# Output projection of a hybrid encoder layer as seven block products, with combinations of the operands formed by GpSimd

## The chip, the cores and the metric

The kernel runs on one NeuronCore of one Trainium2 chip. The metric is the device time in microseconds of one execution. Before the change it is 1117.38 us, the median of three runs (1113.78 to 1118.88).

The engines have their short names: PE is TensorE, DVE is VectorE, ACT is ScalarE, POOL is GpSimd, SP is SyncE. In this kernel nearly all transfers are issued by SP, whose instruction stream is in order: a transfer that must wait for something holds back all those written behind it.

## The reference

One layer on x of 1024 tokens by 1024 features, all in fp32. A combined input projection of the RMS-normalised x feeds three token mixers (a convolution module, a bidirectional retention, and a multi-head latent attention of 8 heads). Their outputs stand side by side, 2048 wide, and are gated. The part that matters here is the end:

```
mix = concat(conv, retention, attention) * silu(gate)     # 1024 tokens x 2048
x   = x + mix @ w_out                                      # w_out: 2048 x 1024
out = rmsnorm(x, final_g)
```

## The kernel before

A matmul of fp32 data is made of three: `mm3` (L174 to 177) splits each operand into a high part, which ACT makes as a cast, and a low part, which DVE makes as the difference, and multiplies high by high, low by high and high by low. So each operand that comes from DRAM costs a transfer on SP, a cast on ACT and a subtraction on DVE before PE can use it.

The kernel has three stages. First the input projection, with the convolution and the retention in its shadow. Then, from about 542 to 943 us, the attention: 16 units (`Unit`, L797 to 863; the loop is L914 to 964), one for each head and each half of the 512 + 512 query tokens, of some 25 us. A unit multiplies queries and keys (L813 to 817), takes the softmax (L820 on DVE, L822 on ACT), transposes the probabilities on PE (`tr`, L831; ACT's cast PH at L833 and DVE's PL empty the bank) and multiplies them by the values (`pvs`). `slot_plan` (L882) puts the projections of the next heads' queries, keys and values between these steps; among them is the rotary part of two heads' queries, `g_r` and `g_r2` (L753 to 776): SP copies rows of `xr` to `xs`, POOL does two multiplications and an addition, ACT casts the result `xh`.

The end of a unit runs while the next one is on. `norm` (L836) loads the gate rows `g`, transposes the softmax sums, stores them to DRAM (`rs_dram`, L846), loads them back broadcast (`rb`, L848), and lets POOL multiply `g` by `rb`. `fin` (L860) lets DVE multiply the unit's result in the bank `pv` by `g` into `osb`, and SP stores it to `y_dram`. `y_dram` holds the transposed mix as 16 tiles of 128 features by 1024 tokens; tiles 0 to 7 are from the convolution and the retention and are complete before the attention, tiles 8 to 15 belong to the 8 heads.

Last comes the output projection (L917 to 1061). `wo_load` loads a tile of w_out (512 KB), casts and splits it; all 16 tiles stay in SBUF. `y_load` loads half of a tile of the mix (256 KB), casts and splits it. There are 8 row tiles of 128 tokens (`st`), 2 column halves, 16 tiles of the contraction and 3 matmuls each: 768 matmuls of 128x512 (of the last row tile one half is cut in two). The first 4 row tiles are started while loads are still coming, and some of their matmuls already stand among the last unit's. `finish` (L1018) adds x, normalises, and stores a row tile.

The order of the instructions on each engine is not the order of the code: when the program is built, a list scheduler with a simulated timeline puts them in order, and the order is then fixed. On the chip each engine goes through its own list and waits on semaphores. Buffers come from pools; `bufs=n` of a tag gives n of them in turn, and a tile waits for the last reader of the one n before it.

## Time and profile before

| | |
|---|---|
| median of three runs | 1117.38 us |
| the profiled execution | 1115.57 us |
| its span in the trace | 1113.8 us |
| mean granted clock of PE | 0.995 |
| PE busy | 1095.9 us, 98% |
| DVE busy | 725.0 us, 65% |
| ACT busy | 412.9 us, 37% |
| POOL busy | 148.9 us, 13% |
| 16 DMA engines, mean | 91 GB/s, 101 MB in all |

The span is the time from the first to the last recorded instruction; the execution's time is 1.77 us longer. A share of busy time is a mean over stages: PE is full nearly throughout, and DVE is fuller in the first stage than in the last. The chain of waits goes back from the last instruction to what released it, step by step, and tells on whose work the end hung. For an engine of which the chain takes little, idle time costs nothing, and added work costs nothing either as long as nobody comes to wait for it.

### The profile page before, as it was taken

What the parts mean: (1) busy time and instruction counts of PE and PEld (TensorE: products, weight loads), DVE (VectorE), ACT (ScalarE), POOL (GpSimd) and SP (SyncE); (2) the same over time, 40 slices, a digit from 0 to 9 for tenths busy, and PEclk for the clock granted to TensorE, in tenths of its full rate; (3) what the DMA queues carried; (4) which work ended last, traced back from release to release, by engine and by line L of the source; (5) the groups of instructions that cost most, each with busy time, mean ns of one, the idle gap of its engine ahead of it and who ended that gap; (6) DMA issues with size and microseconds to landing.
All of it is one profiled execution on the core that took longest, in us unless ns stands there. A gap on an engine that the chain in (4) does not pass through costs nothing.

```text
span 1113.8 us, 14294 instructions
## 1 busy us (share of the span) xinstructions
PE 1095.9 (98%) x5568; PEld 920.2 (83%) x5568; DVE 725.0 (65%) x1011; ACT 412.9 (37%) x741; POOL 148.9 (13%) x135
## 2 busy tenths in 40 slices
PE   9999999999999999999899999999999999999997
PEld 7888888887898899888688888888888877888886
DVE  7599999998747694846865565655555572535033
ACT  8211221121144134324654554554554462424022
POOL 0200000213302442020201101200110000001000
PEclk9999999999999999999999999999999999999999
DMA  7221233221263121226211101211111241835112
GB/s 272 95 64 60 86 103 115 85 87 47 94 210 103 49 76 58 101 79 237 89 36 50 56 34 50 62 34 45 53 55 30 57 142 38 309 97 184 44 45 107
DMA packets 45620, 101.33 MB, mean 91 GB/s; under 512 B 5616, under 2 KB 9568, under 8 KB 45552
## 3 DMA queue, kind: packets, MB, share of 16 engines
q1 hardware_dynamic: 45504, 100.35, 27.2%
q8 instruction: 43, 0.70, 0.3%
q14 instruction: 25, 0.20, 0.1%
q0 software_dynamic: 48, 0.08, 0.0%
HBM read 74.14 MB, written 24.17 MB: 88 GB/s over the span
## 4 chain that ended last, share of the span: by engine, by line
PE 94%; DVE 3%; ACT 1%; DMA 1%; issue 1%; SPq 0%; POOLq 0%; POOL 0%; DVEq 0%; ACTq 0%
PE ps L175 24%; PE ps L176 24%; PE ps L177 24%; PE ps L831 5%; PE ps L813 3%; PE ps L817 3%; PE ps L816 3%; PE ps L814 3%; PE ps L815 3%; PE ps L576 1%; PE ps L565 1%; PE ps L300 1%; PE ps L580 1%; PE ps L578 1%; DMA xh<-lq_dram 0%
## 5 line engine op out<-in xcount | busy, mean ns | idle before, releaser
L176 PE MATMUL ps<-xL,wh 128*128 128x512 f32 (+1 forms) x612 | 238.9, 391 | 0.1
L177 PE MATMUL ps<-xH,wl 128*128 128x512 f32 (+1 forms) x612 | 238.6, 390 | 0.0
L175 PE MATMUL ps<-xH,wh 128*128 128x512 f32 (+1 forms) x612 | 236.3, 393 | 1.7 <-ACT xH L139 1.2
L61 DVE SCALAR_TENSOR_TENSOR acc<-hp,cwh,acc 128x1024 f32<-128x1024 f32 x120 | 154.0, 1323 | 0.1
L175 PEld LDWEIGHTS ps<-xH,wh 128*128 128x128 f32 x612 | 115.1, 189 | 25.5 <-ACT xH L139 1.4
L176 PEld LDWEIGHTS ps<-xL,wh 128*128 128x128 f32 x612 | 115.4, 188 | 24.2 <-DVE xL L61 0.8
L177 PEld LDWEIGHTS ps<-xH,wl 128*128 128x128 f32 x612 | 115.3, 188 | 23.8 <-issue 0.2
L61 DVE SCALAR_TENSOR_TENSOR PL<-ps,PH 128x512 fp32r<-128x512 f32 x128 | 85.6, 684 | 53.0 <-ACT PH L833 52.8
L833 ACT CAST PH<-ps 128x512 fp32r<-128x512 f32 x128 | 73.0, 588 | 92.2 <-PE ps L831 91.6
L176 PE MATMUL ps<-woL,yh 128*128 128x512 f32 (+1 forms) x264 | 100.8, 385 | 0.0
L177 PE MATMUL ps<-woH,yl 128*128 128x512 f32 (+1 forms) x264 | 100.2, 386 | 0.0
L175 PE MATMUL ps<-woH,yh 128*128 128x512 f32 (+1 forms) x264 | 100.0, 386 | 0.0
L820 DVE TENSOR_REDUCE nm<-ps 128x1 f32<-128x1024 f32 x64 | 78.1, 1220 | 31.9 <-PE ps L817 31.2
L166 ACT CAST wh<-wraw 128x1024 fp32r<-128x1024 f32 x40 | 42.1, 1052 | 126.0 <-PE ps L176 116.5
L822 ACT ACTIVATE P<-ps,nm 128x1024 f32<-128x1024 f32 x64 | 71.7, 1120 | 26.6 <-DVE nm L820 24.2
L831 PE MATMUL ps<-ident,P 128*128 128x128 f32 x512 | 72.8, 273 | 0.0
L831 PEld LDWEIGHTS ps<-ident,P 128*128 128x128 f32 x512 | 61.4, 140 | 12.7 <-DVE PL L61 0.8
L61 DVE SCALAR_TENSOR_TENSOR wl<-wraw,wh 128x1024 fp32r<-128x1024 f32 (+2 forms) x45 | 54.3, 1207 | 7.0 <-ACT wh L166 6.1
L813 PE MATMUL ps<-kH,qH 128*128 128x512 f32 x128 | 54.9, 429 | 3.8 <-DVE qL L61 2.6
L176 PEld LDWEIGHTS ps<-woL,yh 128*128 128x128 f32 x264 | 49.7, 188 | 10.3
L177 PEld LDWEIGHTS ps<-woH,yl 128*128 128x128 f32 x264 | 49.6, 188 | 10.2
L175 PEld LDWEIGHTS ps<-woH,yh 128*128 128x128 f32 x264 | 49.7, 188 | 10.0
(292 smaller groups left out, 1984.9 us busy)
## 6 DMA issues: line engine op xcount, KB each, us to landing
wraw<-in_w_in_dram SPq DMA_DIRECT2D x40, 512.0 KB, 3.5
wor<-in_w_out_dram SPq DMA_DIRECT2D x16, 512.0 KB, 4.7
g_dram<-ga SPq DMA_DIRECT2D x29, 256.0 KB, 2.2
yr<-y_dram SPq DMA_DIRECT2D x18, 256.0 KB, 3.7
g<-g_dram SPq DMA_DIRECT2D x16, 256.0 KB, 3.4
rb<-rs_dram SPq DMA_DIRECT2D x16, 256.0 KB, 3.1
y_dram<-osb SPq DMA_DIRECT2D x16, 256.0 KB
z<-in_x_dram SPq DMA_DIRECT2D x8, 512.0 KB, 3.5
```

The lines of the kernel that those rows point to most:

```text
L61: eng.scalar_tensor_tensor(o, a, s, b, op0=op0, op1=op1)
L166: act.copy(hi, t)
L175: pe.matmul(o, sh, mh, start=first, stop=False, skip_group_check=skip)
L176: pe.matmul(o, sh, ml, start=False, stop=False, skip_group_check=skip)
L177: pe.matmul(o, sl, mh, start=False, stop=last, skip_group_check=skip)
L813: pe.matmul(o, qh[:, ts], kh, start=True, stop=False)
L814: pe.matmul(o, qh[:, ts], kl, start=False, stop=False)
L815: pe.matmul(o, ql[:, ts], kh, start=False, stop=False)
L820: dve.tensor_reduce(nm, self.S, axis=AX.X, op=MAX, negate=True)
L822: act.activation(p, self.S, AF.Exp, bias=nm, accum_out=self.rs[:, t:t + 1])
L831: pe.transpose(o[:, c * P:(c + 1) * P], self.p[t][:, (4 * j + c) * P:(4 * j + c + 1) * P], ident)
L833: act.copy(ph, o)
```

## The change

The product of the mix (1024 tokens x 2048) and w_out (2048 x 1024) is cut into 2 x 2 blocks: token halves by halves of the contraction, and halves of the contraction by column halves. The plain way takes 8 products of blocks; the new code takes 7 by a Strassen scheme, of sums and differences of blocks. Each product is 8 contraction tiles by 4 row tiles by 3 matmuls, so 96 matmuls, 672 in all. The products run in the order 1, 7, 2, 6, 4, 5, 3.

- `w_comb(k)`, one in each of units 1 to 8, loads the two tiles k and k+8 of w_out by halves (4 transfers of 256 KB), forms four combinations on POOL, and stores them to `wt_dram` (4 transfers).
- `y_comb(k)`, one in every second unit from 2 to 14 for k = 0 to 6 and one behind the attention for k = 7, does the same for the tiles k and k+8 of the mix, to `yc_dram`. Both use the tag `sc`, 3 buffers of 512 KB.
- `operand` loads one operand tile of 256 KB into the tag `raw` (3 buffers), casts and splits it. Each product has 16 of them, 112 in all, in the place of 16 loads of 512 KB and 32 of 256 KB. The operands lie in two groups of tiles that the products use in turn, so that those of one product can be loaded while PE works on the one before.
- The rows of x are loaded into `z` early; the results of the products 1 and 7 are copied to SBUF by ACT (`pr`); POOL and DVE add them up. `part`, `close` and `store` are the pieces of the old `finish`.

```diff
-            woH = [mk(pa, [P, D], F32R, tag=f"woH{k}") for k in range(NWA)]
...
+            def operand(src_, k, g, tag):
+                t = mk(grp[-1], [P, HS], tag="raw", bufs=3)
+                hi = mk(grp[g], [P, HS], F32R, tag=f"{tag}h{k}")
+                lo = mk(grp[g], [P, HS], F32R, tag=f"{tag}l{k}")
+                sp.dma_start(t, src_)
                 act.copy(hi, t)
                 split_l(dve, lo, t, hi)
-                fg_y[hf, k] = hi, lo
+                return hi, lo
...
+    def w_comb(k):
+        a, b = mk(sx, [P, D], tag="sc", bufs=3), mk(sx, [P, D], tag="sc", bufs=3)
+        for r, t in ((k, a), (k + 8, b)):
+            for n in range(2):
+                sp.dma_start(t[:, half(n)], w_out[r * P:(r + 1) * P, half(n)])
+        b11, b12, b21, b22 = a[:, half(0)], a[:, half(1)], b[:, half(0)], b[:, half(1)]
+        tt(pool, b11, b12, b11, SUB)
+        tt(pool, b12, b22, b12, SUB)
+        tt(pool, b22, b22, b11, SUB)
+        tt(pool, b21, b21, b22, SUB)
+        for i, t in enumerate((a, b)):
+            for n in range(2):
+                sp.dma_start(wt_dram[2 * k + i][:, half(n)], t[:, half(n)])
+
+    def y_comb(k, a, b):
+        a11, a21, a12, a22 = a[:, half(0)], a[:, half(1)], b[:, half(0)], b[:, half(1)]
+        for t, r, hf in ((a11, k, 0), (a21, k, 1), (a12, k + 8, 0), (a22, k + 8, 1)):
+            sp.dma_start(t, y_dram[r][:, half(hf)])
+        tt(pool, a22, a21, a22, ADD)
+        tt(pool, a21, a11, a21, SUB)
+        tt(pool, a11, a22, a11, SUB)
+        tt(pool, a12, a12, a11, SUB)
+        for i, t in enumerate((a22, a11, a21, a12)):
+            sp.dma_start(yc_dram[4 * k + i], t)
...
+            SRC = {1: lambda k: (yo(k, 0), wo(k, 0)), 7: lambda k: (yc(k, 2), wc(k, 1)),
+                   2: lambda k: (yo(k + 8, 0), wo(k + 8, 0)), 6: lambda k: (yc(k, 1), wc(k, 3)),
+                   4: lambda k: (yo(k + 8, 1), wc(k, 2)), 5: lambda k: (yc(k, 0), wc(k, 0)),
+                   3: lambda k: (yc(k, 3), wo(k + 8, 1))}
+            GRP = {1: 0, 7: 1, 2: 0, 6: 1, 4: 0, 5: 1, 3: 0}
...
+            plan = {i: [lambda i=i: pload(1, i)] for i in range(8)}
+        if u >= 1 and u <= 8:
+            plan.setdefault(3, []).append(lambda k=u - 1: w_comb(k))
+        if u >= 2 and u % 2 == 0 and u <= 14:
+            plan.setdefault(6, []).append(lambda k=u // 2 - 1: y_bg(k))
...
+    for k in range(7):
+        pload(7, k)
+    y_comb(7, z[6], z[7])
+    pload(7, 7)
...
+    def product(bank, p, nxt, fresh):
+        for k in range(8):
+            for st in range(4):
+                prod(bank, p, k, st, fresh and k == 0, k == 7)
+            if nxt is not None:
+                pload(nxt, k)
...
+    product(seta, 7, 6, True)
+    for st in range(4):
+        act.copy(p7s[st], seta[st])
...
+    product(setb, 2, 4, False)
...
+    product(seta, 6, 5, True)
...
+    product(setb, 4, 3, True)
...
+    product(seta, 5, None, False)
...
```

The last product, 3, is written row tile by row tile, each with its own end (`part`, `close`, `store`).

Where the instructions now stand. SP from the third unit into the fourth (605 to 628 us in the trace before), from the store of the second unit's result (`y_dram_88`) on. Before, the rotary copies `xs`, the softmax sums `rs_dram` and their return `rb` follow nearly at once:

```order
L863 DMA y_dram_88<-osb_5052 128x512
L839 DMA g_5415<-g_dram_73 128x512
L645 DMA wr_5707<-in_w_uqr_dram 128x384
L762 DMA xs_5166<-xr_5165 32x512 x4
L645 DMA wr_5835<-in_w_uv_dram 128x512
L846 DMA rs_dram_5191<-rr_5194 4x128
L848 DMA rb_5197<-rs_dram_5191 128x512
```

With the change (`sc` are the tiles of the combinations, `yc_dram` and `wt_dram` their stores):

```order
L863 DMA y_dram_88<-osb_5117 128x512
L839 DMA g_5522<-g_dram_73 128x512
L901 DMA sc_5205<-y_dram_88 128x512
L907 DMA yc_dram_118<-sc_5205 128x512
L907 DMA yc_dram_120<-sc_5204 128x512
L907 DMA yc_dram_119<-sc_5204 128x512
L645 DMA wr_5842<-in_w_uqr_dram 128x384
L907 DMA yc_dram_121<-sc_5205 128x512
L888 DMA sc_5376<-in_w_out_dram 128x512 x2
L888 DMA sc_5595<-in_w_out_dram 128x512 x2
L896 DMA wt_dram_106<-sc_5375 128x512
L896 DMA wt_dram_107<-sc_5376 128x512
L888 DMA sc_5596<-in_w_out_dram 128x512 x2
L762 DMA xs_5259<-xr_5258 32x512 x4
```

Before, two rows stand between that store and the copies `xs`; now twelve do, ten of them loads and stores of combinations. `rs_dram` follows behind four more stores, and `rb` behind two more loads.

POOL at the same place. Before, the rotary part of the unit is the only thing between two products `g`:

```order
L64 TENSOR_TENSOR xr_5165<-xr_5165,cosm_4267 128x512
L64 TENSOR_TENSOR xs_5166<-xs_5166,sinm_4268 128x512
L64 TENSOR_TENSOR xr_5165<-xr_5165,xs_5166 128x512
L64 TENSOR_TENSOR g_5188<-g_5188,rb_5197 128x512
```

With the change (of the ten rows of combinations ahead of this `xr`, the last five):

```order
L61 TENSOR_TENSOR sc_5376<-sc_5376,sc_5375 128x512
L61 TENSOR_TENSOR sc_5595<-sc_5595 128x512
L61 TENSOR_TENSOR sc_5376<-sc_5376 128x512
L61 TENSOR_TENSOR sc_5595<-sc_5596,sc_5595 128x512
L61 TENSOR_TENSOR sc_5596<-sc_5596,sc_5595 128x512
L61 TENSOR_TENSOR xr_5258<-xr_5258,cosm_4315 128x512
L61 TENSOR_TENSOR xs_5259<-xs_5259,sinm_4316 128x512
L61 TENSOR_TENSOR sc_5596<-sc_5596 128x512
L61 TENSOR_TENSOR xr_5258<-xr_5258,xs_5259 128x512
L61 TENSOR_TENSOR g_5281<-g_5281,rb_5290 128x512
```

The rotary products and `g` now stand behind combinations that need transfers of their own.

ACT where the last unit ends. After the row `rr` (the softmax sums of the last unit) ACT has, before, only casts of operands:

```order
L845 COPY rr_8073<-ps_8071 4x128
L943 CAST yh_8201<-g_8200 128x512
L931 CAST woH_8173<-wor_8196 128x1024
L931 CAST woH_8174<-wor_8206 128x1024
L943 CAST yh_8211<-yr_8210 128x512
L943 CAST yh_8221<-g_8220 128x512
```

With the change, the four copies of product 1 stand between the second and the third operand of product 7:

```order
L845 COPY rr_8371<-ps_8369 4x128
L959 CAST oyh_8465<-raw_8464 128x512
L959 CAST owh_8471<-raw_8470 128x512
L1044 COPY pr_8455<-ps_8377 128x512
L1044 COPY pr_8456<-ps_8377 128x512
L1044 COPY pr_8457<-ps_8378 128x512
L1044 COPY pr_8458<-ps_8378 128x512
L959 CAST oyh_8477<-raw_8476 128x512
L959 CAST owh_8483<-raw_8482 128x512
```

No cast of a third operand can run before product 1 is complete on PE.

## Rows read from the trace of the kernel before

**Rows 1.** The chain that ended last, by engine.

```profile
PE 94%; DVE 3%; ACT 1%; DMA 1%; issue 1%; SPq 0%; POOLq 0%; POOL 0%; DVEq 0%; ACTq 0%
```

**Rows 2.** Windows in attention and projection: length, busy by engine, clock, DMA share, GB/s.

```profile
core 0: us, PE busy (x) PEld busy (x) DVE busy (x) ACT busy (x) POOL busy (x), PEclk, DMA share, GB/s
541.90:870.00 328.10, 324.53 (x1706) 270.56 (x1705) 193.27 (x276) 173.11 (x331) 44.66 (x35) 1.00 0.15 45
...
943.00:968.00 25.00, 25.00 (x111) 20.57 (x110) 10.40 (x13) 9.10 (x13) 1.29 (x1) 1.00 0.76 272
...
1014.00:1060.00 46.00, 46.00 (x203) 37.93 (x202) 12.50 (x23) 10.33 (x22) 2.75 (x4) 1.00 0.34 115
```

**Rows 3.** Timeline of PE in the projection: start, us, instruction.

```profile
948.27 0.39 PE L177 MATMUL ps<-PH,vL 128*128 128x512 f32 x1
...
957.14 0.39 PE L177 MATMUL ps<-woH,yl 128*128 128x512 f32 x1
...
966.22 0.39 PE L175 MATMUL ps<-woH,yh 128*128 128x512 f32 x1
...
1107.02 0.28 PE L177 MATMUL ps<-woH,yl 128*128 128x256 f32 x1
```

**Rows 4.** Timeline: one load of the mix, from its issue to its split.

```profile
1059.13 0.33 SPq L942 DMA_DIRECT2D yr<-y_dram  x1
...
1062.42 0.62 ACT L943 CAST yh<-yr 128x512 fp32r<-128x512 f32 x1 [1.96 <-DMA yr<-y_dram]
1063.07 0.69 DVE L61 SCALAR_TENSOR_TENSOR yl<-yr,yh 128x512 fp32r<-128x512 f32 x1 [1.88 <-ACT yh L943]
```

**Rows 5.** DMA issues: count, KB each, median us from issue to landing.

```profile
wor<-in_w_out_dram SPq DMA_DIRECT2D x16, 512.0 KB, 4.7
g_dram<-ga SPq DMA_DIRECT2D x29, 256.0 KB, 2.2
yr<-y_dram SPq DMA_DIRECT2D x18, 256.0 KB, 3.7
...
rb<-rs_dram SPq DMA_DIRECT2D x16, 256.0 KB, 3.1
...
z<-in_x_dram SPq DMA_DIRECT2D x8, 512.0 KB, 3.5
```

**Rows 6.** Timeline of the tail: the first and last steps behind the last matmul.

```profile
1107.34 0.42 DVE L64 TENSOR_TENSOR z<-ps,z 128x256 f32<-128x256 f32 x1 [1.44 <-PE ps L177]
...
1110.01 0.81 SPq L1046 DMA_DIRECT2D out_dram<-z  x2
```

**Rows 7.** Groups from 820 us to the end: busy, mean ns of one, by engine.

```profile
L64 POOL TENSOR_TENSOR g<-g,rb 128x512 f32<-128x512 f32 x6 | 7.7, 1289 | 118.0 <-DMA rb<-rs_dram 118.0
...
L64 DVE TENSOR_TENSOR z<-ps,z 128x512 f32<-128x512 f32 x15 | 10.1, 689 | 36.9 <-PE ps L177 34.0 <-DMA z<-in_x_dram 2.9
```

**Rows 8.** Timeline, third and fourth unit: store, rotary part, softmax sums, casts, transposes.

```profile
605.38 0.32 SPq L863 DMA_DIRECT2D y_dram<-osb  x1
...
621.35 1.15 SPq L762 DMA_DIRECT2D xs<-xr  x2
...
626.74 0.27 SPq L846 DMA_DIRECT2D rs_dram<-rr  x1
...
628.34 1.29 POOL L64 TENSOR_TENSOR xr<-xr,xs 128x512 f32<-128x512 f32 x1
...
629.66 0.62 ACT L771 CAST xh<-xr 128x512 fp32r<-128x512 f32 x1 [1.49 <-POOL xr L64]
...
631.59 0.59 ACT L833 CAST PH<-ps 128x512 fp32r<-128x512 f32 x1
...
635.29 1.04 PE L831 MATMUL ps<-ident,P 128*128 128x128 f32 x8
```

**Rows 9.** Timeline of the fifth unit: DVE waits for POOL's gate product.

```profile
656.15 1.29 POOL L64 TENSOR_TENSOR g<-g,rb 128x512 f32<-128x512 f32 x1 [23.30 <-DMA rb<-rs_dram]
657.48 0.69 DVE L64 TENSOR_TENSOR osb<-ps,g 128x512 f32<-128x512 f32 x1 [1.90 <-POOL g L64]
```

**Rows 10.** Windows where PE idled before the attention.

```profile
530.00:540.00 10.00, 6.37 (x30) 4.69 (x30) 9.72 (x16) 6.21 (x12) 0.55 (x1) 1.00 0.40 127
540.00:545.00 5.00, 4.87 (x14) 3.04 (x15) 3.32 (x6) 2.71 (x6) 3.29 (x3) 0.66 0.14 43
```

More of the change, by code (lines that the diff above doesn't have):

```diff
@@ L38 @@
 P_BUFS, PT_BUFS = 3, 2
-NWA = 5
-NYA = 5
 LTB = 3
@@ L100, in body @@
     l_dram = [tc.dram_tile([P, S], F32, name=f"l_dram{i}") for i in range(QT + KVT + 1)]
+    wt_dram = [tc.dram_tile([P, D], F32, name=f"wt_dram{i}") for i in range(16)]
+    yc_dram = [tc.dram_tile([P, HS], F32, name=f"yc_dram{i}") for i in range(32)]
     vec = mk(const, [P, 160], tag="vec")[:, :NV]
@@ L934, in y_load @@
[L934 to L942 removed]
+            grp = [pa]
+            def operand(src_, k, g, tag):
[3 more added lines that the diff above has]
+                sp.dma_start(t, src_)
@@ L943, in y_load, with wo, yo, wc @@
                 act.copy(hi, t)
                 split_l(dve, lo, t, hi)
-                fg_y[hf, k] = hi, lo
-            plan = {1 + k: [lambda k=k: wo_load(k), lambda k=k: y_load(0, k)] for k in range(NWA)}
+                return hi, lo
+            def wo(k, n):
+                return w_out[k * P:(k + 1) * P, half(n)]
+            def yo(k, hf):
+                return y_dram[k][:, half(hf)]
+            def wc(k, i):
+                return wt_dram[2 * k + i // 2][:, half(i % 2)]
+            def yc(k, i):
+                return yc_dram[4 * k + i]
@@ L964, in body @@
         prev = cur
-    SB = [("S",), ("S",), ("pp", "pp"), ("pv", "up")]
-    def bank_pair(i):
-        if i < 2:
-            o = ps("S", 2 * HS)
-            return [o[:, half(c)] for c in range(2)]
-        return [ps(a) for a in SB[i]]
     prev.tr(3, 0)
@@ L975, in body, with prod @@
     prev.norm()
-    ob = [bank_pair(i) for i in range(2)]
-    def wo_mm(st, k, c, a=0, b=HS):
-        yh, yl = fg_y[st // 4, k]
-        ss = slice((st % 4) * P, (st % 4 + 1) * P)
-        cs = slice(c * HS + a, c * HS + b)
-        mm3(ob[st % 4][c][:, a:b], yh[:, ss], yl[:, ss], woH[k][:, cs], woL[k][:, cs], k == 0, k == NG - 1, st == 7)
-    for k in range(NWA):
+    setb = [o[:, half(c)] for o in (ps("S", 2 * HS), ps("S", 2 * HS)) for c in range(2)]
+    def prod(bank, p, k, st, first, last, a=0, b=HS):
+        (yh, yl), (wh, wl) = opd[p, k]
+        ss = slice(st * P, (st + 1) * P)
+        mm3(bank[st][:, a:b], yh[:, ss], yl[:, ss], wh[:, a:b], wl[:, a:b], first, last, True)
+    for k in range(6):
         for st in range(2):
-            for c in range(2):
-                wo_mm(st, k, c)
+            prod(setb, 1, k, st, k == 0, False)
     prev.pvs(0)
@@ new lines, in body, with part @@
+    product(seta, 7, 6, True)
+    for st in range(4):
+        act.copy(p7s[st], seta[st])
+    for st in range(4):
+        sp.dma_start(z[st], x[st * P:(st + 1) * P, :])
+    sp.dma_start(fg, final_g.to_broadcast([P, D]))
+    for st in range(4):
+        tt(pool, p7s[st], p7s[st], p1s[st], ADD)
+    product(setb, 2, 4, False)
+    for st in range(4, 8):
+        sp.dma_start(z[st], x[st * P:(st + 1) * P, :])
+    def part(st, c, bank, i, a=0, b=HS):
+        zc = z[st][:, c * HS + a:c * HS + b]
+        tt(dve, zc, bank[:, a:b], zc, ADD)
+        sq = mk(fin, [P, HS], tag="osb", bufs=2)[:, :b - a]
+        act.activation(sq, zc, AF.Square, accum_out=s2[st][:, i:i + 1])
+        zf = bank[:, a:b] if st == 3 and c == 1 else zc
+        tt(dve, zf, zc, fg[:, c * HS + a:c * HS + b], MUL)
@@ L1040, in finish, with close, store @@
+    def close(st, n):
+        for i in range(1, n - 1):
+            tt(pool, s2[st][:, i:i + 1], s2[st][:, i - 1:i], s2[st][:, i:i + 1], ADD)
+        pool.tensor_scalar(s1[st][:, 0:1], s2[st][:, n - 2:n - 1], 1.0 / D, EPS, op0=MUL, op1=ADD)
+    def store(st, n, bank=None):
+        stt(dve, s1[st][:, 1:2], s2[st][:, n - 1:n], 1.0 / D, s1[st][:, 0:1], MUL, ADD)
+        pool.tensor_tensor(s1[st][:, 1:2], s1[st][:, 1:2], eps_c[:, :1], op=ALU.pow)
         for c in range(2):
-            zf = o2[c] if st == 7 else z[:, half(c)]
+            zf = bank if bank is not None and c == 1 else z[st][:, half(c)]
@@ new lines, in body @@
+    product(seta, 6, 5, True)
+    for st in range(4):
+        zc = z[4 + st][:, half(0)]
+        tt(dve, zc, seta[st], zc, ADD)
+    product(setb, 4, 3, True)
+    for st in range(4):
+        part(4 + st, 0, setb[st], 0)
+        close(4 + st, 2)
+    product(seta, 5, None, False)
+    for st in range(4):
+        part(4 + st, 1, seta[st], 1)
+        store(4 + st, 2)
+    for st in range(4):
+        ch = [(0, HS)] if st < 3 else [(0, 256), (256, HS)]
+        n = 1 + len(ch)
+        for i, (a, b) in enumerate(ch):
+            for k in range(8):
+                prod(seta, 3, k, st, False, k == 7, a, b)
+            part(st, 1, seta[st], 1 + i, a, b)
+            if i == n - 3 or n == 2:
+                close(st, n)
+        store(st, n, seta[st] if st == 3 else None)
```

101 lines of the change are left out of this document (28 added, 73 removed).

## The prediction

> **What bounds the kernel now.** I first read the chain of waits: 94% of the span is PE, so PE's own work sets the end [rows 1]. The windows say where: PE is busy 324.53 of 328.10 us in the attention and without a gap in the projection, at the full clock [rows 2]. The timeline prices a matmul of 128x512 by the distance of starts, not by its duration, since matmuls overlap: 40 of them lie between 957.14 and 966.22 us, 0.227 us each [rows 3]. In the projection DVE and ACT are busy about a quarter of the time and the transfers run well below their peak (last window of [rows 2]). So matmuls taken away there shorten the kernel, as long as operands come fast enough, and work added to POOL, SP, ACT and DVE costs nothing as long as PE never waits for it. The whole prediction is whether these two conditions hold. One thing does not need a forecast: the listed order has 96 matmuls fewer on PE, so the change does what it says. A difference under about 0.5% (5.6 us) can't be told from none for this kernel.
>
> **1. PE's gain.** 96 matmuls x 0.227 = 21.8 us off a stream that ends at 1107.3 [rows 3]. This part is sure; a product takes PE 96 x 0.227 = 21.8 us.
>
> **2. The operands become a ring.** Before, w_out stays in SBUF and the projection loads each operand once, mostly ahead of need. Now each product needs 16 fresh operands of 256 KB, and three `raw` buffers carry them all. A buffer turns like this: issue at 1059.13, cast at 1062.42 (3.29 us later), split from 1063.07 to 1063.76; 4.63 us, and a little for SP to see the end, 4.66 [rows 4]. Three buffers give an operand every 1.555 us, 16 in 24.9 us. PE needs 21.8. So the loads bound every product, 3.1 us each. Only product 1 is loaded inside the attention; the other six, 96 operands, take at least 149 us after it, where PE would need 131. Bounds of the landing, from the nearest rows: 3.7 us for these same loads, 3.1 for `rb`, 2.2 for a store [rows 5]. With 3.1 the turn is 4.46 and a product 23.8, still bound by the loads; with 2.2 it is 3.56 and a product 19.0, and PE sets the pace. I take 3.3, the row of the same transfer in a quiet stretch.
>
> The Trainium skill ("DMA: Bandwidth & Descriptors", section "Anatomy of one DMA — SWDGE (gpsimd) path") fits one transfer, on another path than SP's, as 2.0 us plus its bytes over 436 GB/s, an estimate of 2.6 us for 256 KB. By that a product's loads would take 20.9 us and PE would set the pace; the row shows 3.3 from issue to cast, and no run here shows 2.6 for such a load.
>
> **3. The start of the ring.** In the order on ACT the third operand of product 7 stands behind the four copies of product 1, and these wait until product 1 is done on PE. Before, some 69 projection matmuls were done when the last attention product starts at 948.27 (768 less the (1107.3 - 948.3) / 0.227 = 700 behind it) [rows 3]; now 78 stand ahead of it, so it comes some 2 to 3 us later, near 951, and the last 18 of product 1 end near 956. The copies (0.62 each, as a cast of that size [rows 4]) let the casts go on at about 957; operands 3 to 5 have long landed and are split by 960. The other 11 of product 7 at 1.555 come to 977.
>
> **4. The burst.** While these load, SP also issues eight rows of x (4 MB), the final weights (0.5 MB) and the last combination of the mix (2 MB both ways), with 4 MB of operands. Before, the burst at the same place moved 272 GB/s at a share of 0.76 [rows 2], and a 512 KB load landed in 4.7 us there against 3.5 in quiet [rows 5]. 1.2 us later on each of 11 operands, three at a time, is 4 us; lower bound 0, upper 10. Product 7 is then complete at 981.
>
> **5. The rest of the ring.** 80 operands x 1.555 = 124.4 brings 1106. ACT and DVE also carry copies and sums of the products in their order between casts (some 40 operations of 0.6 to 0.7 us); where they wait for PE they hold the ring. I take 6 us for five boundaries (bounds 0 and 12): 1112. Behind the last operand PE still has 6 whole and 28 half matmuls, 4.8 us: 1116.5. Then the tail: 6.5 us from the last matmul to the end before [rows 3, 6], now with three other row tiles ending together, 8.5: 1125. Against the span of 1113.8 that is 11 us lost, though PE has 22 us less to do.
>
> **6. The attention.** 15 combinations there are 60 loads, 60 stores and 60 operations on POOL of 1.29 us [rows 7], 77 us of POOL in 400, which is no bound by its sum. But SP and POOL go in order. Take the third and fourth unit [rows 8]. The store of `y_dram` is issued at 605.4. The load that reads it back waits for it: 607.6 with a store's 2.2 [rows 5]; it lands 3.4 later, 611; four POOL operations end at 616.2; the last `yc_dram` store has landed at 618.4, and only then can the next loads use its buffer. Their data are in POOL at 621.8, the store of `wt_dram` behind it has landed at 624.0, the next loads go, and the copies `xs` behind them at 625 to 626, 4 to 5 us later than 621.35. POOL then has two more combinations ahead of or between the rotary operations, so `xr` is complete at 635 to 637 instead of 629.6; the cast `xh` waits for it, and behind it on ACT stands PH of 631.59, which must empty a bank before PE's transposes of 635.29. PE waits 3 to 5 us. `rs_dram` and `rb` are some 6 us late as well, so `g`, `osb` and the bank `pv`. DVE's waits for `g` of about 1.9 us cost PE nothing before [rows 9], so about 2 us are free each time. I walked through the other units in the same way: about 5 us in the fourth, 4 for the late `rb` in the fifth and sixth, 4.5 in the seventh and eighth, 0.5 further on, the rest in time. Sum 14 us; lower bound 0, if the hops are shorter than my rows or the slack longer, upper 25, if every one of eight w_out combinations costs 3. The clock may add to that: after PE had been busy 6.37 of 10 us, the stretch behind it was granted 0.66 [rows 10].
>
> **The sum.** 1113.8 - 21.8 of PE's work, + 18.6 for the ring (96 operands at 24.9 a product against 21.8), + 6 at boundaries, + 8 for start, burst and tail = 1125; + 14 in the attention = 1139. The execution's time is 1.8 above its span: **1140 us**. The profiled execution (1115.57) lies 1.8 under the median of the runs, 1117.38; the chances count from the median.
>
> **The rivals.**
> - Loads keep up. Speaks for it: stores of this size land in 2.2 us, so 256 KB can move in less than 3.3. Against: every load of 256 KB on the page takes 3.1 or more [rows 5]. PE then paces: 956 + 6 x 21.8 = 1087, + 5 for the start and the burst, + 8.5 for the tail = 1100 span; with 0 to 14 from the attention the time is 1102 to 1116, at its middle 1106. Faster.
> - The ring binds, but the attention hides the combinations. For: POOL's share stays under a third, the 2 us of slack. Against: the order above. 1125 to 1130, time 1127 to 1131. Slower, by 1%.
> - The attention loses more: the stores that wait for POOL hold SP in each of units 1 to 8, or the clock falls in the gaps. 1125 + 20 to 30: 1147 to 1157.
> - Nothing moves: the ring at 3.1 us of landing (23.8 a product, 12 instead of 18.6) with no loss at boundaries and 4 in the attention: 1113.8 - 21.8 + 12 + 8 + 4 = 1116, time 1118.
>
> **Numbers.** Forecast (1131 to 1147) 0.53; loads keep up 0.13, four fifths of it below 1111.8; attention hides it 0.13; attention loses more 0.13; nothing moves 0.08. So faster by over 0.5% 0.10, within 0.5% 0.10, slower 0.80. The range from 1113 to 1153 leaves out most of the first rival and the upper part of the third, together under 0.2.
>
> **Right or wrong will show** in these places. In the projection PE's busy share should be 0.85 to 0.9 instead of 1, with PE waiting for `owh` (ACT) and `owl` (DVE); a `raw` load should take 3.3 us from issue to cast, and a product 25 us; if PE is full there, step 2 is wrong. In the attention, ACT's cast `xh` and DVE's `osb` should wait for POOL in units four to eight, PE should lose some 14 us of 400, and SP's `xs` should be issued 4 to 5 us late in the fourth unit; if PE is as full as before, step 6 is wrong. The last attention matmul near 965 and the last matmul near 1130 would confirm both.

## The result and the profile after

The changed kernel takes 1158.66 us (median of four runs, 1157.29 to 1162.27) against 1118.01 for the kernel before on the same chip: a ratio of 1.0379, interval 1.0356 to 1.0401. It is slower, as forecast, but by 40.6 us where the forecast had 22, and it lies above the range, which ended at 1153. The profiled execution took 1157.29 us, with a span of 1155.5 and a mean granted clock of 0.979 (before: 0.995).

The page of the changed kernel, busy time by engine, and below it the chain that ended last:

```profile
PE 1097.1 (95%) x5472; PEld 909.9 (79%) x5472; DVE 781.3 (68%) x1079; ACT 448.1 (39%) x813; POOL 260.4 (23%) x215
...
PE 66%; DMA 14%; DVE 6%; POOL 5%; ACT 3%; issue 3%; SPq 1%; POOLq 0%; ACTq 0%; DVEq 0%
```

PE had 94% of the chain [rows 1]. Now transfers, DVE and POOL have a quarter of it: PE waits. Its busy time is as long as before although 96 matmuls are gone, mostly because stretches at a low clock (mean 0.979 against 0.995) lengthen each matmul. The windows say where (columns as in [rows 2]):

```profile
541.90:870.00 328.10, 313.64 (x1610) 258.35 (x1611) 190.80 (x262) 164.56 (x315) 113.93 (x87) 0.99 0.40 130
870.00:943.00 73.00, 66.61 (x339) 54.31 (x339) 47.38 (x66) 38.74 (x74) 14.79 (x11) 0.98 0.40 128
...
968.00:1000.00 32.00, 24.69 (x94) 18.64 (x93) 7.95 (x11) 8.35 (x14) 12.52 (x9) 0.89 0.84 305
1000.00:1050.00 50.00, 44.97 (x178) 33.60 (x177) 34.08 (x36) 23.15 (x43) 21.10 (x15) 0.97 0.55 168
1050.00:1100.00 50.00, 49.32 (x203) 36.64 (x202) 30.23 (x47) 22.37 (x40) 1.00 (x3) 1.00 0.62 180
1100.00:1145.00 45.00, 33.96 (x148) 27.34 (x149) 27.50 (x53) 21.83 (x45) 5.54 (x9) 0.89 0.53 168
```

In the first of them PE is busy 313.64 us where it was 324.53 [rows 2]. In the projection look at the count, not at the busy share: 178 and 203 matmuls in 50 us where before 203 fitted into 46 [rows 2]. The waits of PE name the causes. From 541.9 to 980 us (engine, line, who it waited for: us, times, longest):

```profile
PE ps L831 <- DVE PL L58: 11.5, 5, 5.4
PE ps L813 <- ACT P L822: 2.9, 2, 1.8
PE ps L175 <- DVE kL L58: 2.9, 4, 1.0
PE ps L813 <- DVE qL L58: 2.6, 1, 2.6
```

and from 976 us to the end:

```profile
PE ps L175 <- ACT owh L959: 9.7, 3, 4.0
PE ps L175 <- DVE z L61: 7.7, 1, 7.7
PE ps L176 <- DVE owl L58: 3.1, 10, 0.6
PE ps L175 <- DVE ps L61: 2.6, 1, 2.6
```

`owh` and `owl` are operands of the ring, as forecast. The 7.7 us for `z` are not in the forecast at all: before, PE had no wait there.

How late the attention is shows in `osb`, of which each unit makes one (durations, then first and last start in us). Before:

```profile
L64 DVE TENSOR_TENSOR osb<-ps,g x16: 680/692/692, 580.6 to 948.8; 128x512 f32<-128x512 f32 x16
```

After:

```profile
L61 DVE TENSOR_TENSOR osb<-ps,g x16: 676/691/693, 584.8 to 973.8; 128x512 f32<-128x512 f32 x16
```

The first is 4.2 us late, the last 25.0. I call the difference of such a row to the one before the delay of a unit; it is 11 us at the third unit (unit 2, counted from 0), 17 at unit 12 and 25 at unit 15. Of the 4.2, 1.7 are there before the attention begins, and between profiles of variants that are the same up to there the start differs by several us, so a few us of these delays are of the run and not of the change. The comparisons below take the delay above that of the first unit.

### The profile page after: what moved, and what is told of

Its sections match the earlier page's. It is cut to its first block, busy times and chain, and to the rows that moved or that the text cites. A ratio compares the mean times of both kernels' runs of the same rounds, so it can differ in the third digit from the quotient of the medians.

```text
span 1155.5 us, 14791 instructions
## 1 busy us (share of the span) xinstructions
PE 1097.1 (95%) x5472; PEld 909.9 (79%) x5472; DVE 781.3 (68%) x1079; ACT 448.1 (39%) x813; POOL 260.4 (23%) x215
## 4 chain that ended last, share of the span: by engine, by line
PE 66%; DMA 14%; DVE 6%; POOL 5%; ACT 3%; issue 3%; SPq 1%; POOLq 0%; ACTq 0%; DVEq 0%
PE ps L175 18%; PE ps L176 17%; PE ps L177 17%; PE ps L831 3%; DMA raw<-yc_dram 3%; POOL sc L61 2%; DMA raw<-y_dram 2%; DMA raw<-wt_dram 2%; PE ps L813 2%; PE ps L814 2%; PE ps L817 2%; PE ps L816 2%; PE ps L815 2%; DVE oyl L58 1%; DVE owl L58 1%
## 5 line engine op out<-in xcount | busy, mean ns | idle before, releaser
L175 PE MATMUL ps<-owh,oyh 128*128 128x512 f32 (+1 forms) x232 | 85.1, 403 | 20.6 <-ACT owh L959 9.7
L176 PE MATMUL ps<-owl,oyh 128*128 128x512 f32 (+1 forms) x232 | 94.6, 409 | 3.4 <-DVE owl L58 3.1
L177 PE MATMUL ps<-owh,oyl 128*128 128x512 f32 (+1 forms) x232 | 92.2, 399 | 0.0
L822 ACT ACTIVATE P<-ps,nm 128x1024 f32<-128x1024 f32 x64 | 71.7, 1120 | 25.3 <-DVE nm L820 23.2
L175 PEld LDWEIGHTS ps<-owh,oyh 128*128 128x128 f32 x232 | 44.8, 197 | 34.4 <-ACT owh L959 23.0
L58 DVE SCALAR_TENSOR_TENSOR oyl<-raw,oyh 128x512 fp32r<-128x512 f32 x56 | 45.8, 818 | 36.3 <-ACT oyh L959 36.0
L58 DVE SCALAR_TENSOR_TENSOR owl<-raw,owh 128x512 fp32r<-128x512 f32 x56 | 45.0, 803 | 36.0 <-ACT owh L959 35.6
L61 POOL TENSOR_TENSOR sc<-sc,sc 128x512 f32<-128x512 f32 x37 | 49.5, 1339 | 67.2 <-DMA sc<-y_dram 38.5
L176 PEld LDWEIGHTS ps<-owl,oyh 128*128 128x128 f32 x232 | 45.8, 198 | 19.9 <-DVE owl L58 11.3
```

What stands on the lines that cost most here:

```text
L58: eng.scalar_tensor_tensor(o, a, s, b, op0=op0, op1=op1)
L61: eng.tensor_tensor(o, a, b, op=op)
L175: pe.matmul(o, sh, mh, start=first, stop=False, skip_group_check=skip)
L176: pe.matmul(o, sh, ml, start=False, stop=False, skip_group_check=skip)
L177: pe.matmul(o, sl, mh, start=False, stop=last, skip_group_check=skip)
L822: act.activation(p, self.S, AF.Exp, bias=nm, accum_out=self.rs[:, t:t + 1])
```

## The experiments

All ratios are to the kernel before, on the same chip.

**The ring.** Theory: three `raw` buffers set the pace of the projection. Rival: the transfers are at their limit, or DVE is.

```diff
-                t = mk(grp[-1], [P, HS], tag="raw", bufs=3)
+                if len(grp) > 1:
+                    nraw[0] += 1
+                t = mk(grp[1 if len(grp) > 1 and nraw[0] % 2 else 0], [P, HS], tag="raw", bufs=3)
```

> Edit: the operands of the products 7 to 3 use six raw buffers instead of three. Theory (three buffers of 4.4 to 4.7 us turn set the pace, 23.1 to 26.3 us a product): from product 6 on a product takes PE's 21.8 to 22.5 us, product 7 becomes complete earlier because more loads are under way at once in the burst; 12 to 25 us less than the changed kernel, 1134 to 1147. Rival (casts on ACT and splits on DVE, in order behind other work, or the transfers' own rate set the pace, not the buffers): within 5 us of the changed kernel's 1158.

1130.66 us, 1.0124 (1.0093 to 1.0154): 28 us less, more than expected. The window from 1030 to 1110 us, and the waits of PE from 976 us on:

```profile
1030.00:1110.00 80.00, 80.00 (x354) 66.26 (x353) 61.93 (x103) 46.13 (x89) 7.99 (x14) 1.00 0.66 220
```

```profile
PE ps L175 <- ACT oyh L962: 7.9, 2, 7.1
PE ps L177 <- DVE oyl L58: 3.0, 2, 1.9
PE ps L175 <- DVE ps L61: 1.3, 1, 1.3
```

PE is full at the full clock while the transfers move 220 GB/s, more than the 180 before the edit: they were not at their limit. The 7.7 us for `z` are gone as well, so this edit alone does not price the ring. With four buffers, all in the pool of the old three, it can be priced:

```diff
-                t = mk(grp[-1], [P, HS], tag="raw", bufs=3)
+                t = mk(grp[-1], [P, HS], tag="raw", bufs=3 if len(grp) == 1 else 4)
```

> Edit: four raw buffers behind the attention instead of three, nothing else. Theory (a buffer's turn of 4.5 us over the number of buffers is the pace of the operands: 1.5 us with three, 1.1 with four, and PE takes one every 1.37): four buffers are already faster than PE, so that the products 2 to 3 become bound by PE as with six, and most of the 28 us gained by six are gained: 1131 to 1138. Rival (the gain of six buffers comes from transfers that start earlier, during the last unit, or grows evenly with the number of buffers): 1143 to 1153.

1142.11 us, 1.0237 (1.0222 to 1.0252): 16 us less, 4 short of the range expected. SP's first loads of the products 5 and 3:

```profile
1065.74 0.32 SPq L958 DMA_DIRECT2D raw<-yc_dram  x1
...
1084.15 0.32 SPq L958 DMA_DIRECT2D raw<-yc_dram  x1
```

A product's loads take 18.4 us, three quarters of the 24.6 with three buffers, and PE is full from 1030 to 1090 (60.00 of 60 us busy). One buffer sets the pace or frees it. What stays in this run is the wait at the end:

```profile
PE ps L175 <- DVE z L61: 7.8, 1, 7.8
```

```profile
1090.00:1100.00 10.00, 9.69 (x43) 7.70 (x41) 8.71 (x14) 7.30 (x17) 1.31 (x4) 1.00 0.69 210
1100.00:1110.00 10.00, 2.50 (x6) 2.05 (x7) 8.46 (x16) 4.90 (x12) 0.56 (x1) 0.59 0.35 103
```

So that wait is not the ring's: it came with four buffers too, at the full pace, and behind it the clock fell.

**Is it DVE that POOL slows?** Beside POOL's sums of the products, DVE's splits take longer. With six buffers I moved these sums to DVE, in all three lines that add `p7s` or `p1s`:

```diff
-        tt(pool, p7s[st], p7s[st], p1s[st], ADD)
+        tt(dve, p7s[st], p7s[st], p1s[st], ADD)
```

> Edit: six raw buffers, and the 16 sums of products and x during product 2 and 6 are formed by DVE instead of POOL. Theory (POOL beside DVE makes DVE's splits take 1.7 us instead of 0.69, which costs DVE more than the sums themselves would): the splits of product 2 take 0.69, PE's wait of 1.9 us for one of them goes, DVE is busy less; 1127 to 1130. Rival (DVE's own 11 us of sums delay the splits as much): 1130 to 1134.

1130.39 us, 1.0120 (1.0087 to 1.0154), against 1130.66 with the sums on POOL: no gain. From 1012 to 1034 us (busy us, mean ns of one | idle before), with six buffers, then with the sums on DVE:

```profile
L58 DVE SCALAR_TENSOR_TENSOR oyl<-raw,oyh 128x512 fp32r<-128x512 f32 x8 | 11.0, 1424 | 1.8 <-ACT oyh L962 1.8
```

```profile
L58 DVE SCALAR_TENSOR_TENSOR oyl<-raw,oyh 128x512 fp32r<-128x512 f32 x8 | 5.2, 687 | 0.8 <-ACT oyh L962 0.8
```

The splits are twice as fast, and nothing comes of it. With six buffers there was little to gain: in all PE waited 3.0 us for a split, and 2.0 with the sums on DVE. With three buffers, where a slower split lengthens the turn of the ring, no run tried it.

**The burst.** Theory: the rows of x take the transfers from the operands of product 7. I pinned these loads behind product 7, by a POOL operation on one column of their buffers, which reads product 7's last copy.

```diff
+    def pin(t):
+        tt(pool, t[:, :1], p7s[3][:, :1], p7s[3][:, :1], ADD)
...
+        pin(z[st])
```

> Edit: the loads of x and of the final weights are held back until product 7 has been copied, each by an addition of one column on POOL into the tile that the load then overwrites. Theory (product 7's 16 operands take 40 us instead of 25 because 4.5 MB of x stand among them on SP and in the DMA engines): product 7 takes 28 to 31 us, and part of the gain is given back in product 2, where the loads of x now stand; 1147 to 1154 if half is given back, 1158 if all. Rival (product 7 is late because of the last combination of the mix and the copies of product 1, not of x): no change within 3 us in product 7, 1158 to 1165.

1158.25 us, 1.0371 (1.0330 to 1.0412): nothing. The loads of product 7 took 31 us instead of 38, but those of product 2, now beside x, took 36 instead of 26. With three buffers the ring gives back what one stretch of it gains. With six it does not quite:

> Edit: six raw buffers, as in the run with that edit alone (1130.7), and the loads of x and of the final weights held back until product 7 has been copied. Theory (with the ring gone, what is left of the loss behind the attention is product 7's last operand: it comes from the last combination of the mix, whose loads stand in the burst with x; PE waited 7.1 us there and lost some 4 more to a lower granted clock): 8 to 11 us less, 1120 to 1123. Rival (the burst only moves into product 2, as it did with three buffers): 1128 to 1132.

1125.51 us, 1.0068 (1.0045 to 1.0091), 5 less than with six buffers alone; PE's wait of 7.1 us is 3.0.

**The wait at the end.** Product 3 adds into the banks of product 5; its first matmul waits until DVE has added them to `z`. I gave product 3 the other banks, and DVE adds those of product 5 to `z` beforehand (four more additions).

```diff
-                prod(seta, 3, k, st, False, k == 7, a, b)
+                prod(setb, 3, k, st, k == 0, k == 7, a, b)
```

> Edit: three raw buffers as in the changed kernel; product 3 accumulates in the other set of banks, and DVE adds the sum of the products 6 and 5 to x beforehand (4 more additions on DVE), so that PE needn't wait for the banks of product 5 before it starts product 3. Theory (at the end of the changed kernel PE waits 7.7 us for DVE to empty these banks, with the rows behind splits that wait for loads, and loses the lead it needs; without it the end follows the last operand at about 1134 by 5 us and the tail by 6): 8 to 10 us less, 1148 to 1151. Rival (the wait is only another form of the wait for operands): within 3 us of 1158.

1165.0 us, 1.0405 (1.0369 to 1.0440): no gain. The wait for `z` is gone, but the list scheduler now leaves 30 whole and 48 half matmuls (12.6 us) behind the last operand in place of 9 and 29 (5.5 us), and the clock was 0.55 from 1140 to 1150. The run does not price the wait; it shows that with this ring the end follows the last operand and what is listed behind it.

**The attention.** First without any combination in it (all products then take plain blocks; the last combination, behind the attention, stays):

```diff
-        if u >= 1 and u <= 8:
-            plan.setdefault(3, []).append(lambda k=u - 1: w_comb(k))
-        if u >= 2 and u % 2 == 0 and u <= 14:
-            plan.setdefault(6, []).append(lambda k=u // 2 - 1: y_bg(k))
```

> Edit: the 15 combinations inside the attention are left out altogether, loads, additions on POOL and stores; the products load plain blocks of the same size from w_out and the mix in their place, so the projection computes with other operands. Theory (the combinations in the orders of SP and POOL are what holds the attention up): the last matmul of the attention comes at 950 to 954 instead of 972.6, the rest as in the changed kernel; 1136 to 1141. Rival (the attention is longer because the scheduler placed its other work anew, or because matmuls of product 1 stand in it): no more than 6 us of it go, 1152 or more.

Then with their transfers, but without POOL's operations (`tt(pool, b11, b12, b11, SUB)` and the seven like it are left out, also behind the attention):

> Edit: of the combinations only the additions on POOL are left out (60 in the attention and 4 behind it); their loads and stores stay, so that wrong values are stored and loaded. Theory (the chain of store, load and store that SP goes through in order is most of the delay, POOL's 5.2 us for a combination the smaller part): a third to a half of the 21 us in the attention goes, 1147 to 1152. Rival A (POOL's time, and what it takes from DVE by running beside it, is the delay): nearly all goes, 1137 to 1141. Rival B (POOL doesn't matter): 1156 to 1159.

1144.24 us, 1.0243 (1.0200 to 1.0285), and 1154.84, 1.0342 (1.0308 to 1.0376). Without combinations `osb` is:

```profile
L61 DVE TENSOR_TENSOR osb<-ps,g x16: 679/691/693, 585.4 to 961.9; 128x512 f32<-128x512 f32 x16
```

4.8 us late at the first unit and 13.1 at the last; up to unit 12 it stays at 4.6 to 5.1. So the combinations cost 12 of the 25 us, and 8 are lost in the last units without them, where product 1 is loaded. Both times lie 3 us above what was expected. With the transfers alone the delay at unit 12, above the first unit's, is 5.7 us, with POOL's operations 12.5: about half is the queue of SP, half POOL.

Then the order. The combinations of the mix moved to units 8 to 14, behind those of w_out (with six buffers):

```diff
-        if u >= 2 and u % 2 == 0 and u <= 14:
-            plan.setdefault(6, []).append(lambda k=u // 2 - 1: y_bg(k))
+        if u >= 8 and u <= 14:
+            plan.setdefault(6, []).append(lambda k=u - 8: y_bg(k))
```

> Edit: six raw buffers, and the combinations of the mix moved: k = 0 to 6 in the units 8 to 14, one each, instead of every second unit from 2 to 14; those of w_out stay in units 1 to 8. Theory (a combination costs PE time only where one of w_out and one of the mix share the three sc buffers and SP's order, in units 2 to 8; alone, as in units 10 to 14 of the changed kernel, it costs nothing): the attention loses 2 to 5 us to combinations instead of 12, 1121 to 1125. Rival (each combination costs its own share wherever it stands): 1128 to 1132.

1126.26 us, 1.0083 (1.0057 to 1.0108), 4 less than with six buffers alone, though the intervals touch. All eight combinations of w_out were done by 625 us, though the code spreads them over units 1 to 8: nothing in their operands ties them to a unit, and the scheduler puts them forward. Units 3 to 12 lost nothing more. So I tied them, by a POOL operation on two columns that reads the unit before's `osb` (`o`). With the three buffers of the changed kernel, and the mix again in units 8 to 14:

```diff
+        for t in (a, b):
+            tt(pool, t[:, 0:D:HS], prev.o[:, :2], prev.o[:, :2], ADD)
```

> Edit: the changed kernel with three raw buffers, but each combination is held back until the result of the unit before has been formed (POOL writes two columns of each of its tiles from that result, which the loads then overwrite), and there is one in a unit: w_out in the units 1 to 8, the mix in 8 to 14. Theory (the cost of the combinations is one of their place: the scheduler issues them as early as it can, several behind one another, ahead of rs, rb and xs on SP and of g on POOL): the attention loses no more than without any combination, 13 us against 25; 1144 to 1149. Rival (the cost is their transfers and POOL beside DVE, wherever they stand): 1155 to 1160.

1154.26 us, 1.0346 (1.0313 to 1.0380): 4 us, not the 10 to 15 expected, and not told apart from the changed kernel; the profiled execution is its slowest. Up to unit 7 nothing is lost, at unit 12 it is 7 us: unit 8 has two combinations, one of each kind. The last unit is 26.3 us late, as in the changed kernel: what the first units gain, the last ones lose again. The next runs put the edits together. Six buffers, late x and the mix behind w_out:

> Edit: six raw buffers, x loaded behind product 7, and the combinations of the mix in the units 8 to 14: the three edits that gained alone, together. Theory (they act at different places, ring, burst and attention, so their gains add): attention as in the run with the combinations moved (last unit's result 21 us later than before the change), projection as in the run with x late (150 us): 1120 to 1123. Rival (a gain in the attention is lost again behind it, since the loads of the products set when they can go on): 1125 or more.

1121.83 us, 1.0060 (1.0038 to 1.0083). To that, fewer operands of product 1 in the last unit: six pairs of the eight there, or four, the others behind it.

```diff
-            plan = {i: [lambda i=i: pload(1, i)] for i in range(8)}
+            plan = {2 * i: [lambda i=i: pload(1, i)] for i in range(4)}
...
+    for k in range(4, 8):
+        pload(1, k)
```

> Edit: as the three edits together, and only 6 of the 8 operand pairs of product 1 are loaded inside the last unit, the other two behind it. Theory (of what the attention loses, 8 us fall in the last units even without any combination, where DVE's and ACT's splits and casts of product 1 stand between those of the attention, PE idles and the granted clock falls): 2 to 3 us less than with the three edits, 1118 to 1120. Rival (these 8 us are matmuls of product 1 moved ahead, work that must be done anyway): no change.

> Edit: as the three edits together, but only 4 of the 8 operand pairs of product 1 are loaded inside the last unit, one at every second of its steps, and only their 24 matmuls of two row tiles stand ahead of the last attention product. Theory (as for 6 pairs): the last unit loses 2 to 3 us instead of 8; behind the attention PE has work for 24 matmuls less at once and may wait 2 us for operands: 1116 to 1119. Rival (what is not loaded in the last unit is waited for behind it): 1121 to 1126.

1119.05 us, 1.0038 (1.0015 to 1.0061) with six, 1120.26, 1.0056 (1.0034 to 1.0077) with four: the two are not told apart from each other, nor from the run before them. In PE's order, 48 matmuls of the projection now stand ahead of the last attention matmul with four pairs, and 72 with six, where the changed kernel has 78. To both, the pins:

> Edit: six raw buffers, x late, 4 operand pairs of product 1 in the last unit, and the combinations one in a unit, each held back until the result of the unit before is formed. Theory (place decides): in the first units the loss falls from 14 to 17 us to the 4 to 5 that runs without combinations show; 1120 less 7 to 10 is 1110 to 1114, below the kernel before. Rival (their being decides): 1118 to 1122.

> Edit: as the kernel with one combination in a unit, but with 6 operand pairs of product 1 in the last unit instead of 4. Theory (the splits and casts of product 1 in the last unit cost PE time and clock there): 1 to 4 us more than with 4 pairs, 1112 to 1117. Rival (what is loaded early is gained behind the attention): equal or less.

1112.66 us (12 runs), 0.9967 (0.9950 to 0.9984) with four pairs, and 1116.89 (12 runs), 0.9989 (0.9973 to 1.0006) with six. These ran on another chip than those without pins; by the ratios the pins are worth 0.9% (10 us) with four pairs and 0.5% (5 us) with six. Last, four pairs, pins, and no unit with two combinations:

```diff
-        if u >= 1 and u <= 8:
-            plan.setdefault(3, []).append(lambda k=u - 1: w_comb(k))
-        if u >= 2 and u % 2 == 0 and u <= 14:
-            plan.setdefault(6, []).append(lambda k=u // 2 - 1: y_bg(k))
+        if u <= 7:
+            plan.setdefault(3, []).append(lambda k=u: w_comb(k))
+        if u >= 8 and u <= 14:
+            plan.setdefault(3, []).append(lambda k=u - 8: y_bg(k))
```

> Edit: as the kernel with one combination in a unit and 4 operand pairs in the last (1112.7), but the combinations of w_out one unit earlier (0 to 7), so that no unit has two; before, unit 8 had the last of w_out and the first of the mix. Theory (two close together cost what one in a unit doesn't: DVE waited 4.3 us there): the step of 4 us between the results of units 7 and 9 goes, 1107 to 1110. Rival (a combination of the mix costs this at that place, since it is longer in its waits for stores): 1111 to 1114.

1109.34 us (six runs), 0.9935 (0.9920 to 0.9949): faster than both kernels. (In unit 0, which has no unit before it, the pin reads that unit's own first `p`.) Its page, its last `osb` row and its waits of PE, from 541.9 to 952 us:

```profile
PE 1078.3 (97%) x5472; PEld 905.3 (82%) x5472; DVE 772.0 (70%) x1079; ACT 447.5 (40%) x813; POOL 267.3 (24%) x254
...
PE 81%; issue 5%; DMA 4%; DVE 4%; POOL 3%; ACT 1%; SPq 1%; POOLq 0%; DVEq 0%; ACTq 0%
```

```profile
L61 DVE TENSOR_TENSOR osb<-ps,g x16: 680/690/692, 582.3 to 952.2; 128x512 f32<-128x512 f32 x16
```

```profile
PE ps L813 <- ACT P L822: 3.7, 2, 2.8
PE ps L831 <- DVE PL L58: 3.2, 4, 1.4
PE ps L175 <- DVE kL L58: 3.0, 5, 1.0
```

With the same 15 combinations in the attention, the result of unit 12 is 2.0 us late instead of 16.8, and that of the last unit 3.4 instead of 25.0. Of the latter gain, 6.8 us are only work put off: 30 matmuls of the projection fewer stand ahead of it (48 against 78, 0.227 us each). PE's 21.8 us less still bring only 7.3 by the ratio: in this profile the end is at 1107.3, and the clock 0.991.

## Why the prediction was right in sign and wrong in size

The forecast's own dates against the profile; each stage is counted from the end of the one before.

| | forecast, us | profile, us | difference |
|---|---|---|---|
| last attention matmul | 965 | 972.6 | +7.6 |
| from there to the last operand of product 7 split | 30 | 38.4 | +8.4 |
| 80 operands more | 130.4 | 124.9 | -5.5 |
| from there to the last matmul's end | 4.8 | 13.1 | +8.3 |
| tail | 8.5 | 6.4 | -2.1 |

Together 16.7, from 1139 to the span of 1155.5. Three terms of the sum failed: the start and the burst behind the attention (30 us forecast, 38.4 measured), the 4.8 us behind the last operand (13.1), and the last units of the attention, for which it had nothing (8). That the rest comes out close is partly luck, as steps 2 and 5 show.

- **Step 1, PE's gain:** as forecast in the count (5472 matmuls, of which the projection has 96 fewer) and visible where PE is full. The busy sum does not show it, since the clock fell elsewhere.
- **Step 2, the ring:** right in its mechanism. One turn in product 4, from the issue to the next issue into the same buffer:

```profile
1061.69 0.32 SPq L958 DMA_DIRECT2D raw<-y_dram  x1
...
1064.67 0.62 ACT L959 CAST oyh<-raw 128x512 fp32r<-128x512 f32 x1 [0.88 <-DMA raw<-y_dram]
1065.33 0.69 DVE L58 SCALAR_TENSOR_TENSOR oyl<-raw,oyh 128x512 fp32r<-128x512 f32 x1 [0.81 <-ACT oyh L959]
1066.05 0.32 SPq L958 DMA_DIRECT2D raw<-wt_dram  x1
```

4.36 us, forecast 4.66, since the cast comes 2.98 us after the issue and not 3.3; by three 1.45 per operand, in quiet, or 23.3 a product. Products 2, 6, 4, 5 took 26.3, 24.9, 23.6 and 24.6 us of loads, forecast 24.9: the shorter turn is made up for by holds, the most in product 2, beside which POOL's sums slow the splits. That the ring and nothing behind it is the limit is shown by the two runs with more buffers. The rival "loads keep up" was wrong for the changed kernel; with six buffers it held. (The 20.9 us that the forecast set against it is 21.1 by its own terms, still below PE's 21.8.)
- **Step 3, the start:** not told apart from step 4 by any run, but by the rows. The forecast had five operands of product 7 split 9 us after the last attention matmul (960 against 951); the fifth was split at 985.0, 12.4 after it. The copies of product 1 were done 6 us after it, as forecast (977.98), but the loads were late: SP issued the third only behind the store of the last `osb`:

```profile
974.53 0.32 SPq L863 DMA_DIRECT2D y_dram<-osb  x1
974.90 0.43 SPq L958 DMA_DIRECT2D raw<-yc_dram  x1
```

Its count was off as well: ahead of the last attention matmul PE's rows show some 76 matmuls of the projection before the change, not 69, and 78 after it. So the 2 to 3 us of moved matmuls in this step are not in the result.
- **Step 4, the burst:** mis-sized. The other eleven operands took 26.0 us, against 17.1 at the forecast's quiet pace: 8.9 us where it took 4, with 10 as the upper bound. Its 1.2 us per operand came from the one landing of 4.7 us in [rows 5], and that load was issued behind 968 us, outside the burst of [rows 2]; here the slowest load of the ring landed in 8.7 us. With x late these loads took 31 us instead of 38, so x is most of it. PE had next to no work there:

```profile
985.00:990.00 5.00, 1.02 (x4) 0.56 (x4) 0.40 (x2) 0.62 (x1) 5.00 (x5) 0.83 1.03 419
990.00:995.00 5.00, 5.00 (x12) 3.49 (x11) 1.07 (x2) 1.01 (x2) 3.99 (x3) 0.50 1.04 406
```

PE was busy 1.02 of 5 us, and the next 5 were granted 0.50, which is the level of 1.2 GHz. The transfers were at a share of 1.03, above the 0.76 that the forecast took from the same place [rows 2]. A load of x took 6.3 us where it took 3.5 [rows 5]. The low clock is no term of the 38.4 us, which hang on the loads. That the burst cost the run anything in the end is not shown: the run with x late gained nothing with three buffers.
- **Step 5, boundaries:** the 80 operands took 5.5 us less than 124.4 + 6, by luck. At the quiet turn of 4.36 they would take 116.3, so the ring was held for 8.6 us and not for 6; the shorter turn covers it. **Its end** was wrong: "behind the last operand 4.8 us" priced PE's work alone. At the start of product 3:

```profile
1118.53 0.69 DVE L58 SCALAR_TENSOR_TENSOR oyl<-raw,oyh 128x512 fp32r<-128x512 f32 x1 [1.38 <-ACT oyh L959]
1119.14 0.68 DVE L61 TENSOR_TENSOR z<-ps,z 128x512 f32<-128x512 f32 x1
```

```profile
1119.97 0.77 PE L175 MATMUL ps<-owh,oyh 128*128 128x512 f32 x1 [7.66 <-DVE z L61]
```

The addition that empties a bank of product 5 stands in DVE's order behind splits, and the splits wait for their loads, so PE's first matmul of product 3 waits for operands that it does not need yet. 7.66 us later PE begins a product with a backlog and at half the clock (0.52 from 1120 to 1125). When the last operand is split, at 1135.9, PE comes to it 2.9 us later; from there it has 5.5 us of matmuls, a wait of 2.6 for DVE to empty a bank, and a clock of 0.66 from 1145 to 1150. The parts are read from the rows; no run took this wait alone away, since the one that tried it got another order.
- **Step 6, the attention:** the mechanism was right, in place and size. In the fourth unit, where the forecast had `xs` at 625 to 626, `xr` complete at 635 to 637 and a wait of PE of 3 to 5 us (the starts here are 4.5 us late by what came before):

```profile
630.00 2.41 SPq L762 DMA_DIRECT2D xs<-xr  x4
...
639.72 1.26 POOL L61 TENSOR_TENSOR xr<-xr,xs 128x512 f32<-128x512 f32 x1
641.01 0.62 ACT L771 CAST xh<-xr 128x512 fp32r<-128x512 f32 x1 [5.98 <-POOL xr L61]
...
645.55 1.12 PE L831 MATMUL ps<-ident,P 128*128 128x128 f32 x4 [5.43 <-DVE PL L58]
```

Less the 4.5 us that is 625.5, 636.5 and 5.4. The combinations' 12 us by the run without them agree with the 14 of the forecast. What the forecast left at nothing is the last units: they lose 8 us without any combination too. No moved matmuls are in it (78 ahead of the last attention matmul, some 76 before the change). Before, and without combinations:

```profile
905.00:910.00 5.00, 5.00 (x30) 4.25 (x29) 4.93 (x8) 3.55 (x8) 0.00 (x0) 1.00 0.67 205
910.00:915.00 5.00, 4.50 (x24) 3.35 (x24) 4.50 (x6) 4.07 (x7) 0.00 (x0) 1.00 0.37 104
```

```profile
910.00:915.00 5.00, 2.56 (x9) 1.99 (x10) 5.00 (x9) 4.14 (x8) 0.00 (x0) 0.75 0.86 267
915.00:920.00 5.00, 5.00 (x15) 3.94 (x14) 2.89 (x5) 2.45 (x5) 0.00 (x0) 0.57 0.26 84
```

DVE is nearly full in both, with splits of the first operands among those of the unit. But before, PE had matmuls of the projection to put into its waits from 904.74 us on; without combinations the first one comes at 934.25. From the result of unit 13 to that of unit 14 PE is busy 23.98 of 24.48 us with 120 matmuls before, and 20.58 of 25.52 with 90, at a clock of 0.87, without combinations. Whether the splits or the missing work of PE is the cause, no run separates. Those with four pairs do not: with 30 matmuls fewer ahead, PE idles as long in the last units (7.1 us from the result of unit 12 on in the last run, 4.9 without combinations).
- **The clock:** the forecast wrote that it "may add to that" and put nothing into the sum. It fell to 0.73 between the results of units 13 and 14 (927 to 933 us), to 0.50 in the burst and to 0.50 again ahead of product 3.

The rival "the attention loses more" had the attention at 20 to 30 us. By its time (1147 to 1157) it came nearest, and the last unit's delay of 25 fits it, but only a part of its mechanism: the clock fell in the gaps, and the combinations cost no more than forecast.

## What to carry to other kernels

When operands come through a ring of buffers, count one turn (issue, landing, cast, split) over the number of buffers and set it beside what PE needs in that time: here 4.36 us over three against 1.36 us (21.8 over 16 operands), and one more buffer was worth 16 us, three more 28. Work that is off the bound by its sum still takes its place in in-order queues; a list scheduler puts background work forward to where it holds a queue, and an explicit dependence on the stage's result, one piece a stage, kept it apart (worth 5 to 10 us with six buffers, nothing certain with three). Fewer matmuls are worth their time only if every engine that feeds PE keeps pace up to the last operand: of 21.8 us, the best version here keeps 7.3.

## What the runs showed of the hardware that I had not expected

- DVE's splits and POOL's additions side by side slow each other. From 1007 to 1035 us in the changed kernel:

```profile
L61 POOL TENSOR_TENSOR z<-z,pr 128x512 f32<-128x512 f32 x8 | 13.6, 1732 | 0.0
L58 DVE SCALAR_TENSOR_TENSOR oyl<-raw,oyh 128x512 fp32r<-128x512 f32 x9 | 11.8, 1308 | 3.0 <-ACT oyh L959 2.9
```

1732 ns for POOL where one such operation took 1289 [rows 7], 1308 on average for DVE where it took 690 [rows 4]. With the sums on DVE the splits were back at 687. The Trainium skill ("GPSIMD Engine Reference", section "1. Specifications") says that the two share their SBUF interfaces and contend where a DVE instruction has two SBUF inputs; the trace agrees. With six buffers it cost no time; with three, product 2 is the one beside the sums, and its loads took the longest (26.3 us).
- The loads of the ring, 256 KB each, landed in 2.5, 3.0 and 8.7 us (fastest, median, slowest). The Trainium skill's fit ("DMA: Bandwidth & Descriptors", section "Anatomy of one DMA — SWDGE (gpsimd) path"), weighed in the forecast, gives an estimate of 2.6: the fastest are near it, the median is above it, and the ring bound all the same.
- Gaps of some us in PE's work had stretches at a low clock in or behind them at each place read here: 0.50 from 990 to 995, 0.50 from 1117 to 1120, where PE ran for 0.03 us, and 0.59 from 1100 to 1110 with four buffers. In these places a wait was paid for twice, once as a gap and once as slower matmuls behind it. Not every gap did this: in the last run, from 904 to 928 us, PE was busy 21.71 of 24 us at 1.00.
